# Expert weights laid out tile by tile, ring sizes shifted by one, and results of two expert pairs scattered together

## The chip, the cores and the metric

The kernel runs on one core of one Trainium2 chip. The metric is the device time of one execution in microseconds; the smaller the better.

## What is computed

The reference is a two-layer backbone over 512 latent tokens (and, in the first layer, 256 context tokens) of width 1024, all in float32. Each layer has parallel token mixers and then a mixture of 16 experts in which every expert chooses its tokens. The change touches the mixture only:

```python
def expert_choice_moe(h, w_router, w_g, w_u, w_d):
    cap = (CAP_FACTOR * n) // N_EXPERTS            # 64 of 512 latents, 32 of 256 context tokens
    aff = jax.nn.softmax((h @ w_router).astype(jnp.float32), axis=-1)
    gate, idx = lax.top_k(jnp.swapaxes(aff, 1, 2), cap)
    xe = h[bidx, idx]
    hid = jax.nn.silu(jnp.einsum('becd,edf->becf', xe, w_g)) * jnp.einsum('becd,edf->becf', xe, w_u)
    ye = jnp.einsum('becf,efd->becd', hid, w_d) * gate[..., None].astype(h.dtype)
    return jnp.zeros_like(h).at[bidx, idx].add(ye)
```

A layer's result is `LN(alpha * x + gate * moe)`. In the first layer the experts work on both streams (latents and context), in the second on the latents alone. Per layer the three expert matrices are 16 x 3 x 4 MB, 201 MB, read from HBM once.

## The kernel before

`backbone` writes each layer out in full: the mixers (`mixers`), and then the expert stage, a generator `moe`. Instructions are issued per engine in an order that the tile framework's scheduler settles when the program is built; it may move TensorE instructions past each other where their data allow it.

**The experts' weights.** `ExpertStream` holds one layer's list of loads: 8 pairs of experts, three matrices (0 gate, 1 up, 2 down), four quarters of 256 rows, two experts: 192 tiles of 128 partitions x 2048 floats, 1 MB each. The order is gate 0, up 0, then for each pair the next pair's gate, its own down, the next pair's up. Tiles go round a ring of SBUF buffers, `self.ring`: three "raw" buffers, numbered blocks b0 to b9 that the mixers use too, and, in the second layer, b4, Xc, b10 and three "ew" buffers of pool R. The ring has 13 tiles in the first layer and 18 in the second; the first `early` ones (3 and 5) may be loaded while the mixers still run. `load` issues each tile as one DMA on SP's queue (L1025) from 256 rows of 1024 floats, two rows for each partition; the last pair's down matrix, which is used column half by column half, takes two DMAs a tile. The buffer's earlier reader must be done first.

**The GEMMs.** `gemm(p, mt, ...)` runs over four quarters; in each quarter, latents (L1123) and, in the first layer, context tokens (L1129) are the stationary operand (32 columns in the first layer, 64 in the second) and the weight tile is the moving one, 512 columns a time. One float32 product appears as two matmuls in the trace. After each quarter its two tiles are free and two more loads are issued, and then that quarter's hooks run: small pieces of other work that are put into the GEMM.

**The pairs.** For pair p: the up GEMM, with hooks; the next pair's gate GEMM, with `hidden_T` of this pair as a hook; the down GEMM, with `select` as a hook; then `finish_l` (L1161) and `finish_c`, which scale the result and split it into a high and a low part ("yeh", "yel"; "ych", "ycl").

**The scatter.** A pair's result goes back to its tokens by a multiplication with a permutation matrix ("ptwl", "ptwc"): 8 chunks for the latents and 4 for the context. A chunk (`add_chunk`) is two matmuls of 512 columns into one of two "tr" banks in PSUM (L1176, L1177) and one VectorE operation that adds it to the residual stream (L1184; L1180 for the first pair, L1182 for the last). The 12 chunks of pair p are the hooks of pair p+1's up GEMM, three after each quarter; those of the last pair come at the end, in `last_gemm`.

**Other queues.** POOL gathers the chosen tokens with an indirect DMA (L1087), stores the normalised rows, and in the mixers shuffles the keys (`key_parts`, two DMAs a call). POOL's DMAs use a descriptor scratch in SBUF of the default size.

Of the kernel before, what the change touches and what calls it, by code (L numbers as in the profile page):

```python
# [11 lines left out]
F32R = mybir.dt.float32r  # L12
# [7 lines left out]
L = 2  # L20
D = 1024
KC = 8
NE = 16
# [17 lines left out]
def backbone(ctx: ExitStack, tc: tile.TileContext, A: dict, out: bass.AP):  # L41
    nc = tc.nc
    V, S, G, PE = nc.vector, nc.scalar, nc.gpsimd, nc.tensor
# [948 lines left out]
    class ExpertStream:  # L992
        def __init__(self, l, has_c):
            self.l, self.pool, self.i, self.t, self.has_c, self.stack = l, None, 0, {}, has_c, ExitStack()
            self.ring = [("raw", 3)] * 3 + ([] if has_c else [("b4", 1), ("Xc", 1)])
            self.early = len(self.ring)
            self.ring += [(f"b{i}", 1) for i in (0, 1, 2, 3, 5, 6, 7, 8, 9)]
            self.ring += [("b4", 1)] if has_c else [("b10", 1)] + [("ew", 3)] * 3
            self.size = len(self.ring)
            order = [(0, 0), (0, 1)]  # L1000
            for p in range(8):
                order += ([(p + 1, 0)] if p < 7 else []) + [(p, 2)] + ([(p + 1, 1)] if p < 7 else [])
            self.loads = [(p, mt, qt, e) for p, mt in order for qt in range(4) for e in range(2)]
# [6 lines left out]
        def load(self, upto, after=None):  # L1010
            while self.i < min(upto, len(self.loads)):
                key = p, mt, qt, e = self.loads[self.i]
                tag, bufs = self.ring[self.i % self.size]
                t = T_(self.pool if tag == "ew" else P0, [128, 2, 1024], tag=tag, bufs=bufs)
# [12 lines left out]
                self.i += 1  # L1027

    def moe(l, streams, n2d, st_ew, dst):
        has_c = len(streams) > 1  # L1030
        load_ew, ewt, R = st_ew.load, st_ew.t, st_ew.pool
        load_ew(st_ew.early + (10 if has_c else 7))
        load_ew(st_ew.early + (10 if has_c else 11), streams[0].lgt[:, 0:1])
        XG = block(10, [128, 2, D], F32) if has_c else None
        ng_ = [0]
        for st in streams:
# [65 lines left out]
        lat = streams[0]  # L1102
        cx = streams[1] if has_c else None
# [55 lines left out]
        def finish_l(p, pl):  # L1159
            y = pl.rearrange("p a b -> p (a b)")  # L1160
            V.scalar_tensor_tensor(y, y, lat.gs[p], lat.grow, op0=ALU.mult, op1=ALU.mult)  # L1161
            yh = T_(M, [128, D], F32R, tag="yeh")
            yl = T_(M, [128, D], F32R, tag="yel")
            split(yh, yl, y)
            return combine_l(p, yh, yl)

        def finish_c(p, pc):
            V.scalar_tensor_tensor(pc, pc, cx.gs[p], cx.grow, op0=ALU.mult, op1=ALU.mult)
            ch = T_(M, [128, 512], F32R, tag="ych")
            cl = T_(M, [128, 512], F32R, tag="ycl")  # L1170
            split(ch, cl, pc)
            return combine_c(p, ch, cl)

        def add_chunk(st, p, t, b, pt, rh, rl):
            ps = ps_tr()
            PE.matmul(ps, pt[:, t * 128:(t + 1) * 128], rh, start=True, stop=False)  # L1176
            PE.matmul(ps, pt[:, t * 128:(t + 1) * 128], rl, start=False, stop=True)  # L1177
            xs = st.x1[:, t, b * 512:(b + 1) * 512]
            if p == 0:
                V.scalar_tensor_tensor(xs, xs, ALPHA, ps, op0=ALU.mult, op1=ALU.add)  # L1180
            elif p == 7:
                V.scalar_tensor_tensor(xs, ps, 1.0, xs, op0=ALU.mult, op1=ALU.add, accum_out=st.xsum[:, t, b:b + 1])  # L1182
            else:
                V.tensor_add(xs, xs, ps)  # L1184

        def combine_l(p, yh, yl):
            pt = T_(M, [128, 512], F32R, tag="ptwl")
            V.tensor_copy(pt, lat.PT[p])

            def chunk(t, b):  # L1190
                add_chunk(lat, p, t, b, pt, yh[:, b * 512:(b + 1) * 512], yl[:, b * 512:(b + 1) * 512])

            return [lambda t=t, b=b: chunk(t, b) for t in range(4) for b in range(2)]

        def combine_c(p, ch, cl):
            pt = T_(M, [128, 2, 256], F32R, tag="ptwc")
            for b in range(2):
                V.tensor_scalar(pt[:, b], cx.PT[p], cst[:, C_HALF + b:C_HALF + b + 1], None, op0=ALU.mult)
            return [lambda t=t, b=b: add_chunk(cx, p, t, b, pt[:, b], ch, cl) for t in range(2) for b in range(2)]

        def lhs_x(p):
            return (lambda k, e: lat.xe[p][:, k, 64 * e:64 * e + 64],
# [67 lines left out]
        M = mo.enter_context(pool("M"))  # L1270
# [5 lines left out]
        pend = []  # L1276
        for p in range(8):
            hk = {q: pend[3 * q:3 * q + 3] for q in range(4)}
            if p + 1 < 8:
                hk[2].append(lambda: gather_T(lat, p + 1))  # L1280
                if has_c and p % 2 == 1:
                    hk[3].append(lambda: gather_T(cx, (p + 1) // 2))
            up_gemm(p, sg, hk)
            if p == 0 and has_c:
                cx.grow = T_(M, [128, 512], tag="rowc")
                ada_row_halves(l, 5, cx, cx.grow)
            h = [None, None]
# [12 lines left out]
            if p < 7:  # L1300
                pd, pdc = gemm(p, 2, hT, hTc, hk)
                pend = finish_l(p, pd)
                if has_c:
                    pc = finish_c(p, pdc)
                    pend = [f for i in range(4) for f in (pend[2 * i:2 * i + 2] + pc[i:i + 1])]
# [40 lines left out]
def _layout(inp):  # L1346
    f = {k: np.asarray(v) for k, v in inp.items()}
    c_ = np.ascontiguousarray
    a = {}
# [19 lines left out]
    for k in ("ln1_g", "ln1_b", "ln2_g", "ln2_b", "w_exp_gate", "w_exp_up", "w_exp_down"):  # L1369
        a[k] = c_(f[k])  # L1370
    a["w_router_c"] = c_(f["w_router"].reshape(L, KC, 128, NE).transpose(0, 2, 1, 3))
    cs = np.zeros((128, C_N), np.float32)
    cs[:, C_ID:C_ID + 128] = np.eye(128)
# [11 lines left out]
    t = np.arange(512)  # L1385
# [4 lines left out]
    p = np.arange(128)  # L1390
# [3 lines left out]
    k = np.arange(64)  # L1394
# [7 lines left out]
    for nme, n in (("l", 512), ("c", 256)):  # L1402
        m, j = np.arange(n // 4)[:, None], np.arange(n // 2)[None, :]
# [24 lines left out]
```

## Time and profile before

| | |
|---|---|
| median of 3 runs | 2612.17 us (2610.99 to 2612.55) |
| the profiled execution: time, span | 2609.26 us, 2607.5 us |
| TensorE, VectorE, ScalarE, POOL busy | 2439.2, 1091.3, 723.7, 210.8 us |
| HBM read | 604.53 MB |
| first layer's expert stage | from about 850 to 1490 us of the span |
| second layer's expert stage | from about 2100 us to the end |

The span is from the first to the last instruction of the profiled execution. Matmuls are pipelined, and their ends are modelled: a busy TensorE may still issue below its peak, which is seen from the distance between the starts of its instructions. The DMA share is the mean busy share of the 16 DMA engines; it comes out a little over 1 where they are full.

### The profile page before, as it was taken

The page shows a single profiled execution, that of the slowest core. Times are in us where ns is not written, and L with a number is a line of the kernel's source. Part 1 is how long each engine was busy: PE and PEld are TensorE (multiplying, and loading weights), DVE is VectorE, ACT ScalarE, POOL GpSimd, SP SyncE. Part 2 cuts the span into 40 slices and gives each one's busy share as a digit, 9 for nine tenths or more (in the row PEclk, how much of TensorE's full clock was granted, in tenths as well). Part 3 has the DMA queues.
Part 4 walks back from the last instruction along what each step waited for, and adds up shares of the span by engine and source line. Part 5 has one row for each costly group of instructions (what it writes and reads, how often), then busy time and mean ns, then how long its engine had stood idle before and what let it go on. Part 6 is the DMA issues. An engine that isn't in the chain of part 4 may idle for free. (4 is left out here: it accounts for less than half of the span.)

```text
span 2607.5 us, 35469 instructions
## 1 busy us (share of the span) xinstructions
PE 2439.2 (94%) x14563; PEld 1474.0 (57%) x14563; DVE 1091.3 (42%) x2342; ACT 723.7 (28%) x1400; POOL 210.8 (8%) x247
## 2 busy tenths in 40 slices
PE   6899999999999999999999889999999979988886
PEld 4788876888887333333333277678888733332322
DVE  5656787434337312222221467743433732111214
ACT  4544556322233101010000265532223310000001
POOL 0102121000111000000000012100011100000000
PEclk9999999999999999999999999999999979999998
DMA  7577535222226798878898443552222689999996
GB/s 288 193 265 277 191 109 179 77 81 105 95 73 230 299 395 338 318 305 338 331 355 317 169 140 109 178 206 81 105 97 74 230 345 409 409 409 409 409 409 233
DMA packets 155346, 624.67 MB, mean 240 GB/s; under 512 B 11632, under 2 KB 14064, under 8 KB 137776
## 3 DMA queue, kind: packets, MB, share of 16 engines
q1 hardware_dynamic: 141376, 585.24, 59.5%
q0 software_dynamic: 7520, 23.07, 2.9%
q10 hardware_dynamic: 6288, 14.09, 1.6%
q8 instruction: 114, 1.87, 0.3%
q14 instruction: 48, 0.39, 0.0%
HBM read 604.53 MB, written 10.49 MB: 236 GB/s over the span
## 5 line engine op out<-in xcount | busy, mean ns | idle before, releaser
L1123 PE MATMUL sc<-b,xTl 128*32 128x512 f32 (+1 forms) x2136 | 454.3, 598 | 1.2 <-ACT xTl L286 1.2
L209 DVE TENSOR_TENSOR b<-raw,b 128x512 fp32r<-128x512 f32 x368 | 242.2, 701 | 176.2 <-ACT b L207 171.6
L207 ACT CAST b<-raw 128x512 fp32r<-128x512 f32 x368 | 205.4, 618 | 207.9 <-PE sc L316 122.4
L1123 PEld LDWEIGHTS sc<-b,xTl 128*32 128x32 f32 (+1 forms) x2136 | 119.7, 118 | 202.3 <-issue 197.1
L315 PE MATMUL sc<-b,b 128*128 128x512 f32 x512 | 202.5, 395 | 0.0
L317 PE MATMUL sc<-b,b 128*128 128x512 f32 x512 | 202.0, 395 | 0.0
L316 PE MATMUL sc<-b,b 128*128 128x512 f32 x512 | 202.0, 394 | 0.0
L1123 PE MATMUL sc<-b,hT 128*32 128x512 f32 (+1 forms) x992 | 187.5, 594 | 11.6 <-DMA b<-in_w_exp_down_dram 11.6
L1129 PE MATMUL mm<-b,xTc 128*32 128x512 f32 x776 | 175.1, 593 | 0.3 <-ACT row L273 0.3
L1123 PE MATMUL sc<-raw,xTl 128*32 128x512 f32 (+1 forms) x680 | 157.9, 600 | 0.1
L1161 DVE SCALAR_TENSOR_TENSOR sc<-sc,gsl,row 128x1024 f32<-128x1024 f32 x14 | 18.1, 1292 | 270.8 <-PE sc L1123 270.8
L315 PE MATMUL mm<-b,b 128*128 128x512 f32 (+1 forms) x320 | 123.9, 389 | 3.3 <-DVE lnm L175 2.0
L316 PE MATMUL mm<-b,b 128*128 128x512 f32 (+1 forms) x320 | 123.3, 386 | 0.0
L317 PE MATMUL mm<-b,b 128*128 128x512 f32 (+1 forms) x320 | 122.8, 385 | 0.0
L591 ACT ACTIVATE g<-sc,cst 128x512 f32<-128x512 f32 (+1 forms) x96 | 59.0, 614 | 226.5 <-PE sc L589 226.5
L286 ACT ACTIVATE xTl<-tr,adaC 128x128 f32<-128x128 f32 x64 | 27.5, 455 | 330.8 <-PE tr L1097 166.9
L1184 DVE TENSOR_TENSOR Xl<-Xl,tr 128x512 f32<-128x512 f32 x96 | 62.2, 684 | 135.8 <-PE tr L1177 135.8
L1123 PEld LDWEIGHTS sc<-b,hT 128*32 128x32 f32 (+1 forms) x992 | 52.5, 118 | 103.5 <-issue 79.6
L317 PEld LDWEIGHTS sc<-b,b 128*128 128x128 f32 x512 | 96.3, 188 | 22.7
L316 PEld LDWEIGHTS sc<-b,b 128*128 128x128 f32 x512 | 96.4, 188 | 22.5
L315 PEld LDWEIGHTS sc<-b,b 128*128 128x128 f32 x512 | 96.3, 188 | 22.4
L153 POOL TENSOR_TENSOR rs_b<-rs_a,mhalf 128x1 f32<-128x1 f32 (+2 forms) x85 | 53.8, 633 | 681.9 <-DVE rs_a L151 402.3
(432 smaller groups left out, 4745.4 us busy)
## 6 DMA issues: line engine op xcount, KB each, us to landing
b<-in_w_exp_up_dram SPq DMA_DIRECT2D x87, 1024.0 KB, 10.8
b<-in_w_exp_gate_dram SPq DMA_DIRECT2D x83, 1024.0 KB, 10.8
b<-in_w_exp_down_dram SPq DMA_DIRECT2D x81, 1024.0 KB, 12.4
raw<-in_w_gate_t_dram SPq DMA_DIRECT2D x48, 1024.0 KB, 5.0
raw<-in_w_ada_dram SPq DMA_DIRECT2D x43, 1024.0 KB, 5.3
raw<-in_w_in_t_dram SPq DMA_DIRECT2D x40, 1024.0 KB, 5.2
raw<-in_w_exp_gate_dram SPq DMA_DIRECT2D x27, 1024.0 KB, 8.0
raw<-in_w_exp_up_dram SPq DMA_DIRECT2D x27, 1024.0 KB, 8.7
```

The source lines that it names most:

```text
L153: G.tensor_tensor(r[:, :w], t[:, :w], mhalf[:, :w], ALU.pow)
L207: S.copy(hi[:, c], src[:, c])
L209: V.tensor_sub(lo[:, c], src[:, c], hi[:, c])
L286: S.activation(dst, src, AF.Identity, scale=ada_col(l, ci, st, kc), bias=ada_col(l, si, st, kc))
L315: PE.matmul(ps, hi[:, c, k], h(0, k)[:, :n], start=start and k == k0, stop=False)
L316: PE.matmul(ps, hi[:, c, k], h(1, k)[:, :n], start=False, stop=False)
L317: PE.matmul(ps, lo[:, c, k], h(0, k)[:, :n], start=False, stop=stop and k == k0 + nk - 1)
L591: S.activation(g[:, :n], ps[:, 0, :n], AF.Sigmoid, bias=bgate[l][:, br * 8 + jc:br * 8 + jc + 1])
L1123: PE.matmul(pl[q:q + lw, b, :], lhs_l(k, e)[:, q % 64:q % 64 + lw], weight(p, mt, k, e, b), start=f, stop=s_, tile_position=(0, q))
L1129: PE.matmul(pc[q:q + 32, :], lhs_c(k, e), weight(p, mt, k, e, b), start=f, stop=s_, tile_position=(0, q))
L1161: V.scalar_tensor_tensor(y, y, lat.gs[p], lat.grow, op0=ALU.mult, op1=ALU.mult)
L1184: V.tensor_add(xs, xs, ps)
```

## The change

- On the host, the three expert matrices are laid out tile by tile: each 1 MB tile is one contiguous piece with 8 KB for each partition, the last pair's down matrix in its column halves. Each tile is one DMA, the last pair's too.
- The second layer's ring gets one tile more, "ewx" in pool R, among the early ones: 19 tiles, 6 of them early. The first layer's ring loses b9: 12 tiles.
- In the first layer the chunks of pairs 1, 3 and 5 are held back (`held`) and put together with those of pairs 2, 4 and 6 (`second`): a chunk is then four matmuls into one bank and one VectorE operation, and the 12 chunks run in the hooks of the up GEMM of pairs 3, 5 and 7. The second of the two pairs has result and permutation tiles of its own, its latents' result in b9.
- POOL's descriptor scratch is set to 4096 bytes per partition; the default is 16384.

```diff
-            self.ring = [("raw", 3)] * 3 + ([] if has_c else [("b4", 1), ("Xc", 1)])
+            self.ring = [("raw", 3)] * 3 + ([] if has_c else [("b4", 1), ("Xc", 1), ("ewx", 1)])
             self.early = len(self.ring)
-            self.ring += [(f"b{i}", 1) for i in (0, 1, 2, 3, 5, 6, 7, 8, 9)]
+            self.ring += [(f"b{i}", 1) for i in (0, 1, 2, 3, 5, 6, 7, 8) + (() if has_c else (9,))]
...
-                src = A[("w_exp_gate", "w_exp_up", "w_exp_down")[mt]]
+                dst = t
                 if (p, mt) == (7, 2):
-                    t = t.rearrange("p k (b m) -> p k b m", b=2)
-                    rows, cols = (2 * qt + e) % 4 * 256, (2 * qt + e) // 4 * 512
-                    parts = [(t[:, ex], src[self.l, 2 * p + ex, rows:rows + 256, cols:cols + 512]) for ex in range(2)]
-                else:
-                    parts = [(t, src[self.l, 2 * p + e, qt * 256:(qt + 1) * 256, :])]
-                for dst, rw in parts:
-                    nc.sync.dma_start(dst, rw.rearrange("(k p) m -> p k m", p=128))
+                    dst = t.rearrange("p k (b m) -> p k b m", b=2)
+                nc.sync.dma_start(t.rearrange("p k m -> p (k m)"),
+                                  A[("w_exp_gate", "w_exp_up", "w_exp_down")[mt]][self.l, 2 * p + e, qt])
+                t = dst
...
-        load_ew(st_ew.early + (10 if has_c else 7))
+        load_ew(st_ew.early + (9 if has_c else 7))
...
+            if second(p):
+                yhl = block(9, [128, 2, D])
+                yh, yl = yhl[:, 0], yhl[:, 1]
...
+        def second(p):
+            return "2" if has_c and p % 2 == 0 and p else ""
+
+        def held(p):
+            return has_c and p in (1, 3, 5)
+
-        def add_chunk(st, p, t, b, pt, rh, rl):
+        def add_chunk(st, p, t, b, parts):
             ps = ps_tr()
-            PE.matmul(ps, pt[:, t * 128:(t + 1) * 128], rh, start=True, stop=False)
-            PE.matmul(ps, pt[:, t * 128:(t + 1) * 128], rl, start=False, stop=True)
+            for i, (pt, rh, rl) in enumerate(parts):
+                PE.matmul(ps, pt[:, t * 128:(t + 1) * 128], rh, start=i == 0, stop=False)
+                PE.matmul(ps, pt[:, t * 128:(t + 1) * 128], rl, start=False, stop=i == len(parts) - 1)
...
+        def chunks_of(st, p, nt, parts_of):
+            kept = before.pop(st.name, [])
+            if held(p):
+                before[st.name] = [parts_of]
+                return []
+            fs = kept + [parts_of]
+            return [lambda t=t, b=b: add_chunk(st, p, t, b, [f(b) for f in fs]) for t in range(nt) for b in range(2)]
...
+    def quarters(w):
+        return c_(w.reshape(L, NE, 4, 2, 128, D).transpose(0, 1, 2, 4, 3, 5).reshape(L, NE, 4, 128, 2 * D))
...
-    nc = bacc.Bacc("TRN2", target_bir_lowering=False, num_devices=1)
+    nc = bacc.Bacc("TRN2", target_bir_lowering=False, num_devices=1, dynamic_dma_scratch_size=4096)
```

## Rows read from the trace of the kernel before

**Rows 1.** The page: the span, and DMA use in 40 slices of it.
```profile
span 2607.5 us, 35469 instructions
...
DMA  7577535222226798878898443552222689999996
GB/s 288 193 265 277 191 109 179 77 81 105 95 73 230 299 395 338 318 305 338 331 355 317 169 140 109 178 206 81 105 97 74 230 345 409 409 409 409 409 409 233
```

**Rows 2.** Stretches: length, busy us (count) of each engine, granted clock, DMA share, GB/s.
```profile
10.00:30.00 20.00, 10.74 (x56) 1.08 (x48) 5.68 (x15) 0.20 (x1) 1.10 (x2) 0.95 1.01 418
14.00:26.00 12.00, 7.13 (x40) 0.92 (x40) 2.54 (x5) 0.00 (x0) 0.55 (x1) 1.00 1.02 422
1030.00:1108.00 78.00, 78.00 (x628) 24.95 (x624) 20.13 (x43) 6.01 (x10) 1.87 (x2) 1.00 0.86 331
2040.00:2060.00 20.00, 20.00 (x100) 16.27 (x99) 10.60 (x36) 8.66 (x14) 3.42 (x6) 1.00 0.20 69
2120.00:2540.00 420.00, 377.71 (x1632) 131.45 (x1628) 80.80 (x138) 31.62 (x51) 5.62 (x6) 0.99 1.03 409
```

**Rows 3.** The chain of waits in the second layer's expert stage: start, us, what.
```profile
2262.82 19.10 DMA b<-in_w_exp_down_dram
...
2515.43 18.77 DMA b<-in_w_exp_down_dram
2534.24 3.66 PE sc L1123 x15
...
2601.76 1.28 DVE hT L189
```

**Rows 4.** Groups by line, 985 to 1450: busy us, mean ns, idle before, releasers.
```profile
L1184 DVE TENSOR_TENSOR Xl<-Xl,tr 128x512 f32<-128x512 f32 x44 | 28.2, 683 | 72.2 <-PE tr L1177 72.2
...
L1123 PEld LDWEIGHTS sc<-b,hT 128*32 128x32 f32 x608 | 23.7, 110 | 41.0 <-issue 39.5 <-DMA b<-in_w_exp_up_dram 0.3 <-DMA raw<-in_w_exp_up_dram 0.3
```

**Rows 5.** Timeline of SP around the first GEMM of the second layer's experts.
```profile
2105.42 0.88 SPq L1025 DMA_DIRECT2D ew<-in_w_exp_gate_dram  x2
2115.81 3.80 SPq L1025 DMA_DIRECT2D raw<-in_w_exp_gate_dram  x3
```

**Rows 6.** Timeline of TensorE at the start of the first layer's experts.
```profile
871.00 1.90 PE L1129 MATMUL mm<-b,xTc 128*32 128x512 f32 x10
```

**Rows 7.** Timeline of TensorE around one hook, first layer: start, us, instruction.
```profile
1038.91 0.50 PE L1176 MATMUL tr<-yeh,ptwl 128*128 128x512 f32 x1
...
1039.48 0.40 PE L1176 MATMUL tr<-yeh,ptwl 128*128 128x512 f32 x1
1039.71 0.40 PE L1177 MATMUL tr<-yel,ptwl 128*128 128x512 f32 x1
1040.04 1.04 PE L1123 MATMUL sc<-b,xTl 128*32 128x512 f32 x2
1041.01 0.50 PE L1176 MATMUL tr<-ych,ptwc 128*128 128x512 f32 x1
...
1041.67 1.49 PE L1123 MATMUL sc<-b,xTl 128*32 128x512 f32 x11
...
1046.95 0.50 PE L1176 MATMUL tr<-yeh,ptwl 128*128 128x512 f32 x1
```

**Rows 8.** Timeline of weight loads in a first-layer GEMM, no hook: start, us, instruction.
```profile
993.89 0.13 PEld L1123 LDWEIGHTS sc<-b,xTl 128*32 128x32 f32 x4 [0.30 <-issue]
994.32 0.13 PEld L1123 LDWEIGHTS sc<-b,xTl 128*32 128x32 f32 x4 [0.30 <-issue]
```

**Rows 9.** DMA: a queue (packets, MB, share); issues with count, KB, median us to landing.
```profile
q0 software_dynamic: 7520, 23.07, 2.9%
...
b<-in_w_exp_gate_dram SPq DMA_DIRECT2D x83, 1024.0 KB, 10.8
...
Xl<-Xl POOLq DMA_DIRECT2D x16, 256.0 KB, 3.8
kcE<-kcE POOLq DMA_DIRECT2D x24, 128.0 KB, 3.4
```

More of the change, by code (lines that the diff above doesn't have):

```diff
@@ L1013, in load @@
                 tag, bufs = self.ring[self.i % self.size]
-                t = T_(self.pool if tag == "ew" else P0, [128, 2, 1024], tag=tag, bufs=bufs)
+                t = T_(self.pool if tag[:2] == "ew" else P0, [128, 2, 1024], tag=tag, bufs=bufs)
                 if after is not None:
                     V.tensor_copy(t[:, 0, 0:1], after)
-                src = A[("w_exp_gate", "w_exp_up", "w_exp_down")[mt]]
+                dst = t
                 if (p, mt) == (7, 2):
-                    t = t.rearrange("p k (b m) -> p k b m", b=2)
-                    rows, cols = (2 * qt + e) % 4 * 256, (2 * qt + e) // 4 * 512
-                    parts = [(t[:, ex], src[self.l, 2 * p + ex, rows:rows + 256, cols:cols + 512]) for ex in range(2)]
-                else:
-                    parts = [(t, src[self.l, 2 * p + e, qt * 256:(qt + 1) * 256, :])]
-                for dst, rw in parts:
-                    nc.sync.dma_start(dst, rw.rearrange("(k p) m -> p k m", p=128))
+                    dst = t.rearrange("p k (b m) -> p k b m", b=2)
+                nc.sync.dma_start(t.rearrange("p k m -> p (k m)"),
+                                  A[("w_exp_gate", "w_exp_up", "w_exp_down")[mt]][self.l, 2 * p + e, qt])
+                t = dst
                 self.t[key] = t
@@ L1031, in moe @@
         load_ew, ewt, R = st_ew.load, st_ew.t, st_ew.pool
-        load_ew(st_ew.early + (10 if has_c else 7))
-        load_ew(st_ew.early + (10 if has_c else 11), streams[0].lgt[:, 0:1])
+        load_ew(st_ew.early + (9 if has_c else 7))
+        load_ew(st_ew.early + (9 if has_c else 11), streams[0].lgt[:, 0:1])
         XG = block(10, [128, 2, D], F32) if has_c else None
@@ L1161, in finish_l @@
             V.scalar_tensor_tensor(y, y, lat.gs[p], lat.grow, op0=ALU.mult, op1=ALU.mult)
-            yh = T_(M, [128, D], F32R, tag="yeh")
-            yl = T_(M, [128, D], F32R, tag="yel")
+            if second(p):
+                yhl = block(9, [128, 2, D])
+                yh, yl = yhl[:, 0], yhl[:, 1]
+            else:
+                yh = T_(M, [128, D], F32R, tag="yeh")
+                yl = T_(M, [128, D], F32R, tag="yel")
             split(yh, yl, y)
@@ L1168, in finish_c @@
             V.scalar_tensor_tensor(pc, pc, cx.gs[p], cx.grow, op0=ALU.mult, op1=ALU.mult)
-            ch = T_(M, [128, 512], F32R, tag="ych")
-            cl = T_(M, [128, 512], F32R, tag="ycl")
+            ch = T_(M, [128, 512], F32R, tag="ych" + second(p))
+            cl = T_(M, [128, 512], F32R, tag="ycl" + second(p))
             split(ch, cl, pc)
             return combine_c(p, ch, cl)
-        def add_chunk(st, p, t, b, pt, rh, rl):
+        def second(p):
[3 more added lines that the diff above has]
+        def add_chunk(st, p, t, b, parts):
             ps = ps_tr()
-            PE.matmul(ps, pt[:, t * 128:(t + 1) * 128], rh, start=True, stop=False)
-            PE.matmul(ps, pt[:, t * 128:(t + 1) * 128], rl, start=False, stop=True)
+            for i, (pt, rh, rl) in enumerate(parts):
+                PE.matmul(ps, pt[:, t * 128:(t + 1) * 128], rh, start=i == 0, stop=False)
+                PE.matmul(ps, pt[:, t * 128:(t + 1) * 128], rl, start=False, stop=i == len(parts) - 1)
             xs = st.x1[:, t, b * 512:(b + 1) * 512]
@@ L1184, in add_chunk @@
                 V.tensor_add(xs, xs, ps)
+        before = {}
+        def chunks_of(st, p, nt, parts_of):
[5 more added lines that the diff above has]
+            return [lambda t=t, b=b: add_chunk(st, p, t, b, [f(b) for f in fs]) for t in range(nt) for b in range(2)]
         def combine_l(p, yh, yl):
-            pt = T_(M, [128, 512], F32R, tag="ptwl")
+            pt = T_(M, [128, 512], F32R, tag="ptwl" + second(p))
             V.tensor_copy(pt, lat.PT[p])
-            def chunk(t, b):
-                add_chunk(lat, p, t, b, pt, yh[:, b * 512:(b + 1) * 512], yl[:, b * 512:(b + 1) * 512])
-            return [lambda t=t, b=b: chunk(t, b) for t in range(4) for b in range(2)]
+            return chunks_of(lat, p, 4, lambda b: (pt, yh[:, b * 512:(b + 1) * 512], yl[:, b * 512:(b + 1) * 512]))
         def combine_c(p, ch, cl):
-            pt = T_(M, [128, 2, 256], F32R, tag="ptwc")
+            pt = T_(M, [128, 2, 256], F32R, tag="ptwc" + second(p))
             for b in range(2):
                 V.tensor_scalar(pt[:, b], cx.PT[p], cst[:, C_HALF + b:C_HALF + b + 1], None, op0=ALU.mult)
-            return [lambda t=t, b=b: add_chunk(cx, p, t, b, pt[:, b], ch, cl) for t in range(2) for b in range(2)]
+            return chunks_of(cx, p, 2, lambda b: (pt[:, b], ch, cl))
         def lhs_x(p):
@@ L1304, in moe @@
                     pc = finish_c(p, pdc)
+                if has_c and pend:
                     pend = [f for i in range(4) for f in (pend[2 * i:2 * i + 2] + pc[i:i + 1])]
@@ L1368, in _layout @@
     a["lam_v"] = c_(np.stack([f["lam_q1"], f["lam_k1"], f["lam_q2"], f["lam_k2"]], axis=1))
-    for k in ("ln1_g", "ln1_b", "ln2_g", "ln2_b", "w_exp_gate", "w_exp_up", "w_exp_down"):
+    for k in ("ln1_g", "ln1_b", "ln2_g", "ln2_b"):
         a[k] = c_(f[k])
+    def quarters(w):
+        return c_(w.reshape(L, NE, 4, 2, 128, D).transpose(0, 1, 2, 4, 3, 5).reshape(L, NE, 4, 128, 2 * D))
+    for k in ("w_exp_gate", "w_exp_up"):
+        a[k] = quarters(f[k])
+    down = quarters(f["w_exp_down"])
+    tail = f["w_exp_down"][:, NE - 2:].reshape(L, 2, 4, 2, 128, 2, 512)
+    tail = tail.transpose(0, 5, 2, 4, 1, 3, 6).reshape(L, 4, 2, 128, 2 * D)
+    down[:, NE - 2:] = tail.transpose(0, 2, 1, 3, 4)
+    a["w_exp_down"] = down
     a["w_router_c"] = c_(f["w_router"].reshape(L, KC, 128, NE).transpose(0, 2, 1, 3))
```

## The prediction

> **What bounds the kernel now.** I read the page first: the span is 2607.5 us, and the two expert stages stand out in the line of DMA bytes, one in the middle of the span and one at its end at 409 GB/s [rows 1]. The profiled execution took 2609.26 us, 1.8 us more than its span, and the median of the runs is 2612.17 us, 2.9 us above that. I sum against the span and add 4.7 us at the end.
>
> Then the table by stretches. In the first layer's expert stage TensorE is busy for all of the 78 us of one expert pair while the DMA engines are not (share 0.86). In the second layer's it is the other way round: 409 GB/s through 420 us, at a share of 1.03, TensorE with gaps [rows 2]. The chain of waits agrees: in the second layer each of the later pairs has a DMA piece of about 19 us, the landing of a w_exp_down tile (five such pieces, first and last shown) [rows 3]. In the first layer the groups of lines show two waits of 0.3 us for expert tiles under a group of 608 weight loads [rows 4]. So the first layer's stage is paid in TensorE time and the second's in DMA time; each part of the change is weighed in its own currency.
>
> **Part 1, the tile layout.** Before, an expert tile is 256 rows of 4 KB; after, 128 runs of 8 KB. The bytes are the same. Where the trace moves 8 KB rows with the queue full (the w_ada tiles at the start) it moved 418 GB/s over 20 us, with some small rows among them, and 422 over the middle 12 us, against 409 in the expert stream [rows 2]. I take 420, the middle of the two; the ends are 409 (no gain) and 422.
> What it applies to: the stream of the second layer runs dry once, before 2115.81, when the ring of 18 tiles is full and its next load waits for TensorE to free one [rows 5]. From there it is limited by DMA until 2534.24, when TensorE gets the last tile of the sixth w_exp_down and goes on [rows 3]. That is tile 176 of 192, so 158 tiles of 1.0486 MB, of which 157 with the longer ring. 157 tiles are 164.6 MB: 402.5 us at 409 GB/s, 392.0 at 420: 10.5 us less (0 to 12.4). Gathers and other traffic in that stretch (418.4 us less 405.1 for the 158 tiles, 13 us) I leave as they are.
> After 2534.24 come 73 us until the span's end, in which the chain goes by TensorE, VectorE and ScalarE up to a VectorE piece at 2601.76 [rows 3]; no tile's landing stands in the chain there, so I let the tail move as a whole. In the first layer the same rate gives nothing: nobody waits for it.
> The Trainium skill (DMA: Bandwidth & Descriptors, Why small descriptors are slow) puts a fixed 3 cycles on every packet beside one cycle per 32 bytes. By that, as an estimate, 8 KB packets gain 1.2% over 4 KB ones, some 4.7 us here instead of 10.5. The row says 2.7%, and the row is what I sum.
>
> **Part 2, one ring tile more in the second layer.** It is an early tile: it can load while the DMA engines have room (share 0.20 from 2040 to 2060) [rows 2], so one tile less is left for the saturated stretch: 1.0486 MB at 409 GB/s, 2.6 us less. Ahead of the stretch nothing becomes late: the other tiles keep their order, and the last two are asked for at 2105.42 as before [rows 5]. If it doesn't load early, this part is worth nothing (0 to 2.6).
>
> **Part 3, one ring tile less in the first layer** (block 9 becomes the second pair's result buffer). 12 tiles are six quarters of a GEMM ahead. A quarter issues 48 matmuls of 32 columns at 0.43 us per four [rows 8], 5.2 us; a freed tile is refilled and then used five quarters later, 26 us, and the median landing is 10.8 us [rows 9]. So steady state has 15 us to spare. At the start there is a small loss: while TensorE waits for the latents' gather, it works through the context's matmuls of the first up GEMM, as far as the tiles reach (the 10 matmuls at 871.00 are the last of these) [rows 6]. One tile less takes eight of them out of that idle time: 8 x 0.107 = 0.9 us more (0 if the wait shrinks with it).
>
> **Part 4, two pairs scattered at a time in the first layer.** Before, each pair's 12 chunks (two 512-column matmuls into a "tr" bank and one VectorE add) break into the next up GEMM in four hooks of three. After, pairs 1 and 2, 3 and 4, 5 and 6 share their chunks: four matmuls and one add. The number of matmuls is the same, 36 adds of 0.68 us (24 us) go from VectorE, which is not the bound here, and three of seven up GEMMs lose their hooks. The worth lies in the breaks. One hook from the timeline [rows 7]: the first two chunks take from 1038.91 to 1040.04, 1.13 us where four matmuls at the 0.23 us step (1039.48 to 1039.71) are 0.92; two GEMM matmuls squeezed in take 0.97 us instead of 0.21; the third chunk takes 0.66 instead of 0.46. The GEMM's next 46 matmuls last from 1041.67 to the next hook at 1046.95, 5.28 us where 46 x 0.107 is 4.92. Excess 0.21 + 0.76 + 0.20 + 0.36 = 1.5 us a hook, 6 us a pair. With three of seven sets of four hooks gone and the others no worse: 3 x 6 = 18 us.
> Bounds: the inner break (about 1 us) is there because the third chunk needs the bank that the first one's add frees. With four matmuls a chunk lasts 0.92 us, longer than the 0.68 us add, so the break may vanish from the merged hooks as well: 3 x 10 = 30 us. Or the scheduler, which orders TensorE's instructions by its own model, breaks each merged hook twice: 2.5 us a hook, 3 x 2 = 6 us. I take 18, the hook as it stands in the row. What is late next when 18 us go: the tiles, which have 15 us to spare and need 24 x 2.56 = 61 us of DMA per pair against 78 - 3; they hold. New tiles (second set of result and permutation buffers) are filled while the held pair's are still to be read; the first set is written again only after the merged chunks, as before.
>
> **Part 5, the smaller descriptor scratch.** The POOL queue moved 7520 packets, 40 of its issues are the shuffles of attention's keys [rows 9]; were there no others, that is 188 packets an issue, 12 on each of 16 engines. I cost it at nothing, since its lists are short; its price, if that is wrong, is the last rival.
> The Trainium skill (DMA: Bandwidth & Descriptors, SWDGE vs HWDGE vs iDMA) says that GpSimd writes its descriptors to rings in a reserved part of SBUF, so a quarter of that part is a rule that speaks against the change. No row of before shows POOL short of room.
>
> **The sum.** 2607.5 - 10.5 - 2.6 + 0.9 - 18 = 2577.3 us of span, plus 4.7: **2582 us**.
>
> **The rivals.**
> 1. *The merged hooks break twice* (part 4 at 6 us): 2594. For it: in the row the scheduler already puts two matmuls between chunks. Against: the longer chunk hides the add.
> 2. *The breaks go altogether* (30 us): 2570.
> 3. *The expert stream stays at 409 GB/s*: the 8 KB rows at the start stood alone, with little compute beside them, and part 1 gives nothing: 2592.5. Together with rival 1: 2604.5. The Trainium skill's 3-cycle rule (part 1) would end at 2588, inside the forecast's own range.
> 4. *POOL waits for descriptor room*: slower than before. In attention each call of key_parts issues two POOL DMAs back to back (24 of 3.4 us and 16 of 3.8 us to landing, 20 calls) [rows 9]. If the scratch held only one, the second would be issued after the first has landed: 20 x 3.6 = 72 us where nothing covers it, 2654; it beats the 30 us gain from the point where more than 30 of the 72 are uncovered. Against: at most 12 packets an engine and issue, by the count above.
>
> **How the numbers follow.** About 0.2% (5 us) is what a measurement of this kernel can tell from no change. Forecast 0.55 (2575 to 2589); rival 1, 0.15; rival 2, 0.08; rival 3, 0.10, with rival 1, 0.05; rival 4, 0.05; gains eaten by a new order of the instructions around the layers' borders, 0.02. Faster 0.93, the same 0.02, slower 0.05. The range runs from all gains at their upper ends (12.4 + 2.6 + 30, 2567) to rivals 1 and 3 together (2604), so 2566 to 2604.
>
> **What would show it.** Right: about 418 to 420 GB/s in the long stretch of the second layer, its first refill of a freed tile with 19 tiles already loaded, DMA pieces of some 17 us still in the chain; in the first layer a pair of periods some 6 us shorter where the chunks were merged, up GEMMs of pairs 2, 4 and 6 with no chunk, 0.69 us adds down by 36, and the tail after the last w_exp_down tile unchanged at 73 us. Wrong: 409 GB/s again; merged hooks with more than one run of GEMM matmuls inside; waits for expert tiles in the first layer; POOL's issues drawn apart in attention.

## The result, and the profile after

| | before | after |
|---|---|---|
| median | 2612.36 us (2610.99 to 2613.26, 4 runs) | 2571.99 us (2566.62 to 2575.01, 4 runs) |
| ratio | | 0.9844 [0.9827, 0.9861] |
| profiled execution: time, span | 2609.26, 2607.5 us | 2571.94, 2570.1 us |

The kernel is 40 us faster; 30 were forecast. The page of the changed kernel first (span, then DMA use and GB/s in 40 slices), to be held against [rows 1]:

```profile
span 2570.1 us, 35398 instructions
...
DMA  7577635223224698979899333562322589999995
GB/s 286 188 271 275 213 107 185 73 71 115 90 82 171 278 420 316 388 296 386 329 360 374 140 136 111 174 216 71 119 82 82 207 347 420 421 420 421 421 418 245
```

In the second layer 409 became 420 to 421. The same stretches as in [rows 2] (us from the start, length, busy us and count of PE, PEld, DVE, ACT, POOL, granted clock, DMA share, GB/s):

```profile
1030.00:1108.00 78.00, 78.00 (x695) 25.18 (x688) 16.02 (x34) 7.47 (x12) 1.87 (x2) 1.00 0.98 385
2120.00:2520.00 400.00, 367.09 (x1575) 128.91 (x1576) 85.63 (x146) 29.28 (x49) 5.95 (x6) 0.99 1.01 420
```

In the first layer TensorE is still busy for the whole 78 us and issues 695 matmuls in them where it issued 628. But this window now lies on GEMMs almost without hooks, so that step is not the gain. Over two whole pairs (from scaling to scaling, marks below; before, then after) the matmuls are the same and the time is shorter:

```profile
1112.78:1271.55 158.77, 158.77 (x1278) 51.22 (x1274) 38.80 (x73) 13.82 (x24) 2.81 (x3) 1.00 0.85 327
1099.89:1250.09 150.20, 150.20 (x1278) 51.60 (x1274) 31.36 (x61) 13.78 (x24) 3.10 (x3) 1.00 0.89 345
```

The timeline of TensorE around a merged hook shows why, beside [rows 7] (start, us, line, out<-in, count):

```profile
1105.77 0.50 PE L1184 MATMUL tr<-yeh,ptwl 128*128 128x512 f32 x1
1106.11 0.39 PE L1185 MATMUL tr<-yel,ptwl 128*128 128x512 f32 x1
1106.34 0.40 PE L1184 MATMUL tr<-b,ptwl 128*128 128x512 f32 x1
...
1107.49 0.39 PE L1185 MATMUL tr<-b,ptwl 128*128 128x512 f32 x1
1107.75 0.50 PE L1184 MATMUL tr<-ych,ptwc 128*128 128x512 f32 x1
...
1108.55 0.40 PE L1185 MATMUL tr<-ycl,ptwc 128*128 128x512 f32 x1
1108.88 1.92 PE L1120 MATMUL sc<-b,xTl 128*32 128x512 f32 x16
...
1114.16 0.50 PE L1184 MATMUL tr<-yeh,ptwl 128*128 128x512 f32 x1
```

Twelve scatter matmuls run in one piece of 3.11 us (2.76 at the 0.23 us step), and the GEMM's next 48 matmuls take 5.28 us to the next hook (5.14 at 0.107). Before, the hook of [rows 7] had a run of two GEMM matmuls inside. The piece only just holds: the third chunk starts at 1107.75, and VectorE's add that frees its bank ends 0.06 us earlier:

```profile
1107.00 0.69 DVE L1192 TENSOR_TENSOR Xl<-Xl,tr 128x512 f32<-128x512 f32 x1 [2.92 <-PE tr L1185]
```

From here on hooks are compared by periods between two fixed marks.

The marks are VectorE's scaling of a pair's result (L1161 before, L1158 after), whose first element comes when a down GEMM ends. Timelines of VectorE, before and then after; first pairs 2 and 4 of the first layer, then pairs 0 and 6 of the second:

```profile
1112.78 1.29 DVE L1161 SCALAR_TENSOR_TENSOR sc<-sc,gsl,row 128x1024 f32<-128x1024 f32 x1 [8.24 <-PE sc L1123]
1271.55 1.29 DVE L1161 SCALAR_TENSOR_TENSOR sc<-sc,gsl,row 128x1024 f32<-128x1024 f32 x1 [8.44 <-PE sc L1123]
2171.09 1.29 DVE L1161 SCALAR_TENSOR_TENSOR sc<-sc,gsl,row 128x1024 f32<-128x1024 f32 x1 [9.28 <-PE sc L1123]
2537.92 1.29 DVE L1161 SCALAR_TENSOR_TENSOR sc<-sc,gsl,row 128x1024 f32<-128x1024 f32 x1 [31.03 <-PE sc L1123]
```

```profile
1099.89 1.29 DVE L1158 SCALAR_TENSOR_TENSOR sc<-sc,gsl,row 128x1024 f32<-128x1024 f32 x1 [8.24 <-PE sc L1120]
1250.09 1.29 DVE L1158 SCALAR_TENSOR_TENSOR sc<-sc,gsl,row 128x1024 f32<-128x1024 f32 x1 [8.44 <-PE sc L1120]
2149.70 1.29 DVE L1158 SCALAR_TENSOR_TENSOR sc<-sc,gsl,row 128x1024 f32<-128x1024 f32 x1 [9.28 <-PE sc L1120]
2502.77 1.29 DVE L1158 SCALAR_TENSOR_TENSOR sc<-sc,gsl,row 128x1024 f32<-128x1024 f32 x1 [29.54 <-PE sc L1120]
```

Two pairs of the first layer took 158.8 us and take 150.2. Six pairs of the second took 366.8 and take 353.1. With three further marks (VectorE's product of up and gate of pair 0 and of pair 7 in the first layer, and the threshold of the second layer's top-k, L968) the span of every kernel of this case falls into stretches. Each figure below is a difference of two starts in the profiled execution:

| us | up to pair 0's product | to pair 0's scaling | first layer: to pair 7's product | to the second layer's top-k | to its pair 0 | stream: to its pair 6 | to the end |
|---|---|---|---|---|---|---|---|
| before | 906.5 | 47.6 | 503.0 | 642.7 | 71.3 | 366.8 | 69.5 |
| after | 906.3 | 46.4 | 477.4 | 648.0 | 71.5 | 353.1 | 67.4 |
| e1 layout alone | 909.5 | 47.6 | 503.0 | 642.5 | 71.5 | 355.7 | 67.9 |
| e2 merge alone | 904.7 | 46.4 | 477.5 | 646.7 | 70.6 | 366.9 | 68.0 |
| e3 ring tile alone | 907.3 | 47.6 | 503.1 | 642.6 | 71.1 | 364.3 | 68.0 |
| e4 after, no merge | 909.9 | 46.4 | 503.1 | 646.3 | 71.5 | 353.1 | 67.3 |
| e5 bank held | 904.9 | 46.4 | 486.7 | 646.5 | 71.1 | 353.1 | 67.5 |
| e6 rows of 4 KB | 904.2 | 46.4 | 477.5 | 646.9 | 71.6 | 364.6 | 65.8 |
| e7 three pairs | 910.5 | 46.4 | 483.1 | 645.9 | 71.0 | 353.2 | 69.0 |
| e8 junk in SBUF | 902.3 | 46.4 | 477.5 | 643.7 | 71.4 | 353.1 | 67.7 |
| e10 two ring tiles | 915.4 | 46.4 | 477.5 | 641.3 | 71.6 | 350.6 | 66.4 |
| e11 scratch 2048 | 905.7 | 46.4 | 477.5 | 643.1 | 70.6 | 353.2 | 66.1 |
| e12 rows of 2 KB | 904.2 | 46.4 | 477.5 | 646.8 | 70.3 | 388.0 | 65.8 |

This table carries most of what follows. Three columns repeat to 0.2 us wherever what bounds them is the same: the second, the third and the stream. The first (mixers, attention and the first GEMMs) differs by 13 us between profiles, the fourth by 1.5 to 2.4 between like kernels (after, e2, e5, e6, e12; e8, e10, e11), the fifth by about 1, the last by 4. That is the noise of one execution, and it makes the columns that repeat sharper than any median. From before to after: -0.2, -1.2, -25.6, +5.3, +0.3, -13.8, -2.2, in sum -37.3.

### The profile page after: what moved, and what is told of

It reads as the page before. It is cut to its first block, busy times and chain, and to the rows that moved or that the text cites. A ratio compares the mean times of both kernels' runs of the same rounds, so it can differ in the third digit from the quotient of the medians.

```text
span 2570.1 us, 35398 instructions
## 1 busy us (share of the span) xinstructions
PE 2410.0 (94%) x14563; PEld 1473.7 (57%) x14563; DVE 1068.1 (42%) x2306; ACT 723.7 (28%) x1400; POOL 212.9 (8%) x247
## 3 DMA queue, kind: packets, MB, share of 16 engines
q1 hardware_dynamic: 87872, 585.24, 59.0%
## 5 line engine op out<-in xcount | busy, mean ns | idle before, releaser
L1120 PE MATMUL sc<-b,xTl 128*32 128x512 f32 (+1 forms) x2208 | 414.8, 595 | 2.4 <-ACT xTl L286 2.4
L1120 PEld LDWEIGHTS sc<-b,xTl 128*32 128x32 f32 (+1 forms) x2208 | 112.4, 117 | 193.7 <-issue 186.1
L1120 PE MATMUL sc<-b,hT 128*32 128x512 f32 (+1 forms) x824 | 165.1, 594 | 2.5 <-DMA b<-in_w_exp_down_dram 2.5
L1126 PE MATMUL mm<-b,xTc 128*32 128x512 f32 x808 | 155.9, 592 | 0.3 <-ACT row L273 0.3
L1120 PE MATMUL sc<-raw,xTl 128*32 128x512 f32 (+1 forms) x608 | 135.1, 605 | 0.6 <-ACT xTl L286 0.6
L1158 DVE SCALAR_TENSOR_TENSOR sc<-sc,gsl,row 128x1024 f32<-128x1024 f32 x14 | 18.1, 1293 | 258.7 <-PE sc L1120 258.7
L596 POOL TENSOR_TENSOR Xl<-Xl,g 128x512 f32<-128x512 f32 x48 | 63.3, 1319 | 514.1 <-DVE g L595 514.1
L595 DVE TENSOR_TENSOR g<-g,sc 128x512 f32<-128x512 f32 (+1 forms) x72 | 42.8, 594 | 147.0 <-ACT g L591 147.0
```

What stands on the lines that cost most here:

```text
L595: V.tensor_mul(g[:, :n], g[:, :n], ps[:, 1, :n])
L596: G.tensor_add(m[:, jc, :n], m[:, jc, :n], g[:, :n])
L1120: PE.matmul(pl[q:q + lw, b, :], lhs_l(k, e)[:, q % 64:q % 64 + lw], weight(p, mt, k, e, b), start=f, stop=s_, tile_position=(0, q))
L1126: PE.matmul(pc[q:q + 32, :], lhs_c(k, e), weight(p, mt, k, e, b), start=f, stop=s_, tile_position=(0, q))
```

## The experiments

The median of the kernel before was 2610.8 us beside e1 to e4, 2608.6 beside the others; so kernels of different groups are compared by their ratios to it.

**e1: the layout alone.** The kernel before with the host's tiles and the one DMA a tile, ring and hooks as they were.

```diff
-                    parts = [(t, src[self.l, 2 * p + e, qt * 256:(qt + 1) * 256, :])]
...
+                nc.sync.dma_start(t.rearrange("p k m -> p (k m)"),
+                                  A[("w_exp_gate", "w_exp_up", "w_exp_down")[mt]][self.l, 2 * p + e, qt])
...
```

> The new tile layout alone (8 KB runs, the last pair's tiles in one DMA each), rings, scratch and scatter as before. Theory: the second layer's long stretch runs at 420 GB/s in place of 409, some 11 us less over its 158 tiles, and 1 to 2 us less in the tail: about 2600 us; the first layer is unchanged within 1 us. Rival (the stream stays at 409, the gain of the changed kernel's end came from elsewhere): 2612.

Measured: 2598.83 us (2596.86 to 2600.31), ratio 0.9959 [0.9942, 0.9975]; by this ratio 10.7 us less. The stream is 11.1 us shorter, every other column that repeats is unchanged.

**e2: the merge alone**, with the first layer's ring of 12 and the small scratch, the old layout, 18 tiles in the second layer.

```diff
+            return has_c and p in (1, 3, 5)
...
+                PE.matmul(ps, pt[:, t * 128:(t + 1) * 128], rl, start=False, stop=i == len(parts) - 1)
```

> The merged scatter alone, with b9 out of the first layer's ring and the small scratch; tiles of 4 KB rows and 18 ring tiles in the second layer as before. Theory (the inner breaks vanish from merged hooks): 8.5 us less for each of the three merged sets, 26 us by the end of the seventh up GEMM, and some 4 to 5 us given back at the layers' border: about 2590. Rival (a hook costs what it cost before, only fewer of them): 18 us less by then.

Measured: 2586.07 us (2582.60 to 2587.87), 0.9913 [0.9897, 0.9929]; by this ratio 22.7 us less. Up to pair 7's product the first layer gained 25.5, and 4.0 came back before the second layer's top-k.

**e3: the ring tile alone**, with the small scratch.

```diff
-            self.ring = [("raw", 3)] * 3 + ([] if has_c else [("b4", 1), ("Xc", 1)])
+            self.ring = [("raw", 3)] * 3 + ([] if has_c else [("b4", 1), ("Xc", 1), ("ewx", 1)])
...
-    nc = bacc.Bacc("TRN2", target_bir_lowering=False, num_devices=1)
+    nc = bacc.Bacc("TRN2", target_bir_lowering=False, num_devices=1, dynamic_dma_scratch_size=4096)
```

> One early ring tile more in the second layer and the small scratch, all else as before. Theory: one tile less in the saturated stretch, 2.6 us less: 2609.8, with 19 tiles loaded before the first is freed. Rival (the tile isn't loaded early, or the last tiles aren't what the end waits for): the same as before. If POOL lacked room, attention would be longer by more than 1 us.

Measured: 2606.78 us (2600.45 to 2610.75), 0.9987 [0.9977, 0.9997]: a gain so small that the interval just leaves out none. The stream has it plainly: 364.3 instead of 366.8 us, 2.5 less for one tile.

**e4: everything but the merge.** Ring of 12, block 9 out, new layout, 19 tiles; every pair scattered by itself.

```diff
-            return "2" if has_c and p % 2 == 0 and p else ""
+            return ""
...
-            return has_c and p in (1, 3, 5)
+            return False
```

> The changed kernel with the merge undone: every pair scattered in the next up GEMM, the first layer's ring still 12 tiles. Theory: the inner breaks are back, 22 us slower than the changed kernel: about 2594, with no wait for expert tiles in the first layer and not over 1 us for the missing ring tile at its start. Rival (the short ring costs more than that and hides part of the merge's worth): 2597 or more, with tile waits in the first layer.

Measured: 2598.54 us (2594.41 to 2600.33), 0.9955 [0.9937, 0.9972]. The first layer is back at 503.1 us and the stream keeps its 353.1: the two gains are independent. But from pair 7's product to the top-k it takes 646.3 us, not the 642.7 of before. So most of what is given back there (3.6 of 5.3 us) comes with the ring of 12 and not with the merge; e1 and e3, which keep 13 tiles in the first layer, don't show it, and e2 does. No run changed that ring alone, so this is by elimination. The time lies above the 2594 expected and above the rival's 2597, but the rival's cause is missing: no wait for an expert tile in the first layer is longer than 0.4 us, and the 503.1 us are those of before.

**e5: the bank held as long as before, relative to a chunk.** The changed kernel; after each add VectorE copies the same bank once more into a tile that nobody reads, so a bank comes free 1.3 us after its chunk instead of 0.7.

```diff
                 V.tensor_add(xs, xs, ps)
+                if has_c:
+                    V.tensor_copy(T_(M, [128, 512], tag="held"), ps)
```

> The changed kernel, and in the first layer each scatter's bank is held longer: after the add a second VectorE operation copies it to a spare tile (pairs 1 to 6). Theory (the inner break comes when the bank isn't free within the length of a chunk): an add and a copy take some 1.3 us, more than the 0.92 us of a merged chunk, so GEMM matmuls or idle time stand inside the merged hooks again, about 1 us a hook, 12 us in all: 2584. Rival (the breaks are fewer because the hooks are fewer, whatever the bank does): 2572, merged hooks still in one piece of 3.1 us.

Measured: 2579.60 us (2578.09 to 2581.12), 0.9884 [0.9864, 0.9904], by the ratios 10.4 us above the changed kernel. Two pairs take 153.3 us (150.2 after, 158.8 before). The timeline of TensorE around a hook of this kernel:

```profile
1106.10 0.39 PE L1185 MATMUL tr<-b,ptwl 128*128 128x512 f32 x1
1106.42 1.04 PE L1120 MATMUL sc<-b,xTl 128*32 128x512 f32 x2
1107.40 0.50 PE L1184 MATMUL tr<-ych,ptwc 128*128 128x512 f32 x1
...
1108.20 0.39 PE L1185 MATMUL tr<-ycl,ptwc 128*128 128x512 f32 x1
1108.52 1.49 PE L1120 MATMUL sc<-b,xTl 128*32 128x512 f32 x11
```

The inner break of [rows 7] is back, two GEMM matmuls for 0.98 us, and so are the GEMM runs cut as before (11 after the hook, not 16). In 11 of the 12 merged hooks a chunk's weight load now waits for the copy. It costs 3.1 us a set of four hooks, 9.3 in three sets (column three: 486.7 against 477.4). That splits the merge's 25.6 us: 9.3 because the inner breaks are gone, and the remaining 16.3 because there are half as many hooks. My 2584 had put 12 us on the breaks, a little much; the rival's 2572 is excluded.

**e6: rows of 4 KB in the same tiles.** The changed kernel; each contiguous 1 MB tile is read as 256 rows of 4 KB, the two halves of a partition in the opposite order, which the host has swapped, so that rows cannot run together.

```diff
-                nc.sync.dma_start(t.rearrange("p k m -> p (k m)"),
-                                  A[("w_exp_gate", "w_exp_up", "w_exp_down")[mt]][self.l, 2 * p + e, qt])
+                nc.sync.dma_start(t[:, ::-1],
+                                  A[("w_exp_gate", "w_exp_up", "w_exp_down")[mt]][self.l, 2 * p + e, qt].rearrange("p (k m) -> p k m", k=2))
...
```

> The changed kernel, with each contiguous 1 MB tile moved as two 4 KB rows per partition in swapped order, so that 4 KB rows come from the same addresses. Theory (the length of a row sets the rate): 409 GB/s in the second layer's long stretch, 11 us slower than the changed kernel: 2583. Rival (the order of addresses in HBM does it, two rows of a partition 512 KB apart before, neighbours now): 420 GB/s and 2572.

Measured: 2579.00 us (2578.43 to 2582.22), 0.9885 [0.9869, 0.9902], 0.41% above the changed kernel's ratio or 10.7 us. Stream 364.6 us, what e3 had. The rows did stay apart: the page counts 137024 packets on the weights' queue where the changed kernel has 87872, which is 128 more for each of the 384 tiles. So the gain is the length of the rows; that a tile is one contiguous megabyte adds nothing.

**e12: rows of 2 KB**, as e6 with four parts.

```diff
-                nc.sync.dma_start(t.rearrange("p k m -> p (k m)"),
-                                  A[("w_exp_gate", "w_exp_up", "w_exp_down")[mt]][self.l, 2 * p + e, qt])
+                nc.sync.dma_start(t.rearrange("p k (c m) -> p (k c) m", c=2)[:, ::-1],
+                                  A[("w_exp_gate", "w_exp_up", "w_exp_down")[mt]][self.l, 2 * p + e, qt].rearrange("p (k m) -> p k m", k=4))
...
```

> The changed kernel, the same contiguous 1 MB tiles, each read as rows of 2 KB in the opposite order (the host swaps them, so the values are the same). From 409 GB/s at 4 KB and 420.5 at 8 KB over 16 DMA engines a row takes 160.3 and 311.7 ns, that is 8.9 ns and 37.0 ns per KB. Theory (a fixed time for each row): 2 KB rows take 84.6 ns, 387 GB/s, the stream of layer 2 is 353 x 420.5 / 387 = 383.6 us, and the time 2602. Rival (the rate at 2 KB is the 401 GB/s that the window of the last tiles of the kernel before shows): stream 370, time 2589. Rival 2 (row length doesn't matter below 4 KB): 409, stream 364.5, time 2582 to 2583.

Measured: 2601.69 us (2600.90 to 2604.53), 0.9975 [0.9962, 0.9988]. The long stretch of the second layer in e6, then in e12 (columns as above):

```profile
2120.00:2520.00 400.00, 360.84 (x1540) 126.50 (x1537) 80.65 (x136) 28.04 (x45) 5.95 (x6) 0.99 1.03 409
```

```profile
2120.00:2520.00 400.00, 348.70 (x1470) 120.30 (x1468) 76.80 (x132) 27.03 (x44) 5.95 (x6) 0.99 1.05 387
```

The 387 GB/s were worked out beforehand from 409 and 420.5 with a fixed 8.9 ns a row; the 401 of the kernel before's last tiles was no measure of it. The stream took 388.0 us where 383.6 were expected, and why it is 4.4 us longer was not tried. The time came out as expected, at 2602, in part by luck: beside this run the kernel before took 3.8 us less than beside the changed kernel.

**e7: three pairs scattered at a time** (pairs 1 to 3, 4 to 6), with blocks 7 and 8 as result buffers and a first-layer ring of 10.

```diff
...
-            return "2" if has_c and p % 2 == 0 and p else ""
+            return ("3", "", "2")[p % 3] if has_c and 0 < p < 7 else ""
...
-            return has_c and p in (1, 3, 5)
+            return has_c and p in (1, 2, 4, 5)
```

> The changed kernel with three pairs scattered at a time in the first layer (1 to 3, 4 to 6), their buffers taken from b7 and b8, so a ring of 10 tiles. Theory: one more set of four hooks goes, 8.5 us less by the end of the seventh up GEMM: about 2563, if five quarters of cover (ten tiles) still bring every tile in time. Rival (the ring is too short): waits for expert tiles in the first layer, at least as many us lost as won, 2572 or more.

Measured: 2579.21 us (2576.90 to 2580.84), 0.9880 [0.9863, 0.9896]: slower than two at a time. Two lines of its timeline, one from long before the third pair's result is there, one from when it comes:

```profile
1144.57 0.47 PE L1187 MATMUL tr<-yeh,ptwl 128*128 128x512 f32 x1 [0.36 <-DVE gsl L1064]
...
1180.00 0.73 PE L1187 MATMUL tr<-b,b 128*128 128x512 f32 x2 [1.54 <-ACT b L201]
```

The first matmuls of a chunk, for whose pairs the results were long there, were issued alone between GEMM runs, and a chunk's last ones wait 1.54 us for the third pair's split: a bank is opened early and finished late. Of the first set's four merged hooks the first is broken up by this; the other three run in one piece. The first layer takes 483.1 us instead of 477.4, where 8.5 us less were expected. The rival's cause is excluded: the only wait for an expert tile in the first layer is one of 0.2 us. With the ring of 10 and the buffers changed at once, this run doesn't say which of them made that order; it says that the merge doesn't simply go on paying.

**e8: the junk output of the context's final norm in SBUF.** The squares that `affine_norm` writes only for their sum went to a PSUM pair "sc" (L186); here they go to a free SBUF tile.

```diff
-            junk = ps_sc().rearrange("p a b -> p (a b)")
+            junk = T_(M, [128, D], tag="sg") if has_c and st.s else ps_sc().rearrange("p a b -> p (a b)")
```

> The changed kernel, with the discarded output of the context's last norm in the first layer written to SBUF and not to the pair of PSUM banks that the last GEMM's first half needs. Theory: the 3.5 us in which TensorE waits there go, about 2568.5. Rival (VectorE and ScalarE have the norms to do in any case and the wait only moves): 2572.

Measured: 2566.26 us (2563.88 to 2569.05), 0.9836 [0.9820, 0.9853]. The last GEMM in the changed kernel, then one line each of e4 and of the kernel before, then its beginning in e8:

```profile
1455.64 0.40 PE L1185 MATMUL tr<-ycl,ptwc 128*128 128x512 f32 x1
1459.53 7.09 PE L1146 MATMUL sc<-b,hT 128*64 128x512 f32 x32 [3.49 <-ACT sc L186]
1472.82 1.22 PE L1184 MATMUL tr<-yeh,ptwl 128*128 128x512 f32 x2 [6.21 <-ACT yeh L201]
```

```profile
1488.09 8.78 PE L1146 MATMUL sc<-b,hT 128*64 128x512 f32 x32 [3.49 <-ACT sc L186]
```

```profile
1478.26 3.22 PE L1149 MATMUL mm<-b,hT 128*64 128x512 f32 x13
```

```profile
1431.40 0.60 PE L1250 MATMUL tr<-cst,sgc 128*128 128x128 f32 x4
1431.93 1.07 PE L1146 MATMUL sc<-b,hT 128*64 128x512 f32 x2
1432.94 1.05 PE L1126 MATMUL mm<-b,hTc 128*32 128x512 f32 x2
```

In the changed kernel the half that goes to "sc" waits 3.49 us for the norm to leave the bank, with nothing else left to issue; in e4 the same row shows the same 3.49. The wait, of 3.3 to 3.5 us, stands in every kernel with the ring of 12 and the junk in PSUM (e2, e5, e6 and e12 too). It stands in none with the ring of 13 (before, e1, e3): in the kernel before the other half's matmuls lay there (13 of them, from 1478.26 on). It stands in none with the junk in SBUF (e8, e10, e11), and in e7, with the ring of 10, it is 0.4 us. In e8 the half that goes to "sc" runs first, and the stretch to the top-k falls from 648.0 to 643.7 us. By the medians the step from after to e8 is 0.08%, inside both intervals; by the stretch it is 4.4 us, more than that column's noise.

**e10 and e11: the scratch halved again, and a second ring tile.** e11 is e8 with 2048 bytes of scratch; e10 puts a tile "ewy" into the room that this frees.

```diff
-            self.ring = [("raw", 3)] * 3 + ([] if has_c else [("b4", 1), ("Xc", 1), ("ewx", 1)])
+            self.ring = [("raw", 3)] * 3 + ([] if has_c else [("b4", 1), ("Xc", 1), ("ewx", 1), ("ewy", 1)])
...
-    nc = bacc.Bacc("TRN2", target_bir_lowering=False, num_devices=1, dynamic_dma_scratch_size=4096)
+    nc = bacc.Bacc("TRN2", target_bir_lowering=False, num_devices=1, dynamic_dma_scratch_size=2048)
```

> The changed kernel with the junk in SBUF and the scratch for GpSimd's descriptors halved once more (2048 bytes), nothing else. Theory (the room for descriptors bounds nothing here): 2566 as with 4096, and the attention stages up to the first router's top-k within the 4 us by which they differ between profiles. Rival (GpSimd waits for room): more than 4 us later at that top-k and 2572 or more.

> The changed kernel with the context's final-norm junk in SBUF, the scratch for GpSimd's descriptors at 2048 bytes a partition instead of 4096, and in the room that this frees a second added ring tile in the second layer. The stream of layer 2 (first pair's scaling to the seventh's) took 366.8 us before, 364.3 with one tile more, 353.1 in the changed kernel. Theory (the stream bounds layer 2 and each tile that is loaded before it costs 1 MB less at 420 GB/s): stream 350.6, time 2.5 us below the kernel with the junk in SBUF, so 2563.8. Rival (the early tiles no longer fit in the time in front of the stream, or GpSimd waits for descriptor room): no gain or a loss, 2566 or more.

Measured: e11 2564.41 us (2563.34 to 2571.28), 0.9836 [0.9823, 0.9850]; e10 2567.32 (2562.71 to 2570.93), 0.9834 [0.9820, 0.9847]. The scratch bounds nothing at an eighth of its default either: e11's first column is 905.7 us. In e10's profile that column is 915.4, but e7 and e4, with twice the scratch, have 910; e11 with the same scratch doesn't show it. The second tile does what the first did, 350.6 us of stream against 353.1, and the runs' medians don't resolve it (2563.8 was expected). e8, e10 and e11 are the fastest kernels of this case, each some 0.1% below the changed one by ratio, which their intervals don't separate from it.

## Why the prediction was right, and where it was off

The forecast was 2582 us by four terms; 2572 came. It lies in the wide range, under the forecast's own range of 2575 to 2589, and 2 us from the 2570 of rival 2, which had a chance of 0.08. That the sum missed by only 10 us is in part luck: part 4 gave 7.6 us more than its term, and 5.3 us came back at the layers' border, for which the sum had no term; the two partly cancel.

- *What bounds what*: right. The two gains add up (e1, e2, e4), one in TensorE's time, the other in DMA time.
- *Part 1* (-10.5): right in size and cause. e1 -11.1, and e6 takes 11.5 back. Rows of 2 KB moved 8.0% less than rows of 8 KB, 387 against 420.5 GB/s (e12). The Trainium skill's fixed 3 cycles a packet (DMA: Bandwidth & Descriptors, Why small descriptors are slow) would, as an estimate, have given 4.7 us here and a loss of 3.4% for 2 KB rows. The trace agrees with a fixed cost a row, not with its size.
- *Part 2* (-2.6): right, -2.5 in e3, once more in e10. The tile loads early, at 2002.31, as was assumed; SP's timeline of the changed kernel has it long before the first refill that waits for TensorE beside [rows 5]:

```profile
2002.31 0.33 SPq L1020 DMA_DIRECT2D ewx<-in_w_exp_gate_dram  x1
...
2094.41 3.76 SPq L1020 DMA_DIRECT2D raw<-in_w_exp_gate_dram  x3
```

- *Part 3* (+0.9): wrong in sign and place. The loss at the start didn't come: that stretch is 1.2 us shorter in every kernel with a ring of 12, and waits for tiles stay at 0.3 us or less each, 1.7 us of weight loads together (1.3 before). The ring's price stood at the stage's other end, +3.6 us (e4), where the order of the last GEMM's matmuls changed and its first half ran into the norm's bank (e8). The step took the ring for a question of transfers alone; that the scatter, the norm and the last GEMM share the PSUM banks "tr" and "sc" was not looked at. Why a ring of 12 leads to that order is not shown.
- *Part 4* (-18): the mechanism was right, the term mis-sized: -25.6. I priced a merged hook "as it stands in the row", inner break included. e5 shows the two halves: 16.3 us for half the hooks (18 in the sum), and 9.3 for inner breaks that vanished, since a chunk of four matmuls (0.92 us) outlasts the add (0.69 us). That sentence stood in the bounds; the 1 us of rival 2's breaks measures 0.77 a hook. The adds fell as counted: in the groups by line, 985 to 1450 as in [rows 4], the latents' 44 became 24 (the code has 48 and 24 of these in the first layer), with 12 for the context:

```profile
L1192 DVE TENSOR_TENSOR Xl<-Xl,tr 128x512 f32<-128x512 f32 x24 | 16.5, 687 | 47.7 <-PE tr L1185 47.3
...
L1192 DVE TENSOR_TENSOR Xc<-Xc,tr 128x512 f32<-128x512 f32 x12 | 8.2, 687 | 3.6 <-PE tr L1185 3.3
```

- *Part 5* (0): right, and e11 at half of it too. POOL's shuffles land in 4.2 and 3.8 us where they landed in 3.8 and 3.4 [rows 9], and in the first layer, from the top-k of the context's router to that of the latents' (with the attention between them), it is 523.1 us, 523.6 before.
- *Tail "as a whole"*: 2.2 us shorter, but kernels with the old layout have 68.0 too; within this column's noise.
- *DMA pieces of some 17 us in the chain*: wrong. There are six, of 20 to 21 us; the first and the last:

```profile
2334.78 21.02 DMA ewx<-in_w_exp_gate_dram
...
2479.19 19.86 DMA Xc<-in_w_exp_down_dram
```

They begin at 2334.78 where [rows 3] began at 2262.82: TensorE lives longer on what was loaded before. The first five follow one another almost without TensorE between them (2334.78 to 2438), which the five of before, one a pair, did not. Why each piece is longer was not tried.

Of the rivals, three are excluded: 1 (no run of GEMM matmuls in a merged hook), 3 (420, not 409) and 4 (e11). Rival 2 is what happened to the hooks in kind; its 2570 overstated them (30 against 25.6). The case with the small chance, gains eaten at the layers' borders, is there as well: 5.3 us, of which e4 puts 3.6 on the ring and e8 recovers 4.4; the rest, 1.7 us, is not more than that column's noise and stays open.

## What to carry to other kernels

Cost a hook in a GEMM by what breaks it, not by its instructions: the same matmuls cost 25.6 us less in 12 whole hooks than in 24 broken ones, and a hook broke again when its bank was freed later than the next chunk was due (e5). For a weight stream at the DMA bound, lay each tile out so that a partition's share is one row, and take the fixed cost a row from two row lengths of the same kernel. After a change in buffers, look at the end of the stage too: an output that nobody reads can hold the one bank that the last GEMM needs.

## What was not expected of the hardware

- Three row lengths lie on one line: 2, 4 and 8 KB rows moved at 387, 409 and 420.5 GB/s, which over 16 DMA engines is 8.9 ns a row and 37.0 ns per 1000 bytes; the rate at 2 KB was worked out before it was run.
- Two of the GEMM's 32-column matmuls between 128-column scatter matmuls take 0.97 us before [rows 7] and 0.98 in e5, where two in a long run take 0.21. The next chunk's weight load comes after the same idle time whether the profile names the bank as its releaser (e5, second line) or nothing (before, first line; the add that frees the bank ended at about 1040.3):

```profile
1041.01 0.19 PEld L1176 LDWEIGHTS tr<-ych,ptwc 128*128 128x128 f32 x1 [0.84 <-issue]
1107.39 0.19 PEld L1184 LDWEIGHTS tr<-ych,ptwc 128*128 128x128 f32 x1 [0.84 <-DVE held L1194]
```

  So in the hook of before it was the short piece that cost the time, not a wait on the chip for the bank. The bank acts through the order that the scheduler settles when the program is built: where it is held longer, the short piece is there again (e5). A change to scatter matmuls and back around a long run is cheaper: the merged hook and the 48 matmuls behind it have 0.5 us together over their steps.
- The stretch up to the first mark, nearly the same code in every kernel, took between 902 and 915 us in the profiled executions, while the experts' stretches repeat to 0.2 us; differences of a few us are read from stretches, not from spans.
